# Hybrid stream step on one core: the first four columns projected without the adaLN shift, which is added to their results

## The chip, the cores and the metric

The kernel runs on one core of a Trainium2 chip. The metric is the device time of one execution in microseconds (us). Before the change it is 1371.86 us, the median of 3 runs (1371.81 to 1372.82).

## The reference, cut to what matters

One layer of an encoder is computed for 512 prompt rows and 64 sample rows (576 rows, 1024 channels). The two groups have their own conditioning vector c, and so their own shift, scale and gate.

```python
def layer(x, c, ...):
    mod = (jax.nn.silu(c) @ w_ada + b_ada)[:, None, :]
    sh1, sc1, gt1, sh2, sc2, gt2 = jnp.split(mod, 6, axis=-1)
    h = rms_normalize(x) * g_norm_mix * (1.0 + sc1) + sh1
    q, k, v, qi, ki, wi, z, xbc, dt, gate_logits = jnp.split(h @ w_in, offs, axis=-1)
    ...
    g_attn, g_ssm = jnp.split(jax.nn.sigmoid(gate_logits), 2, axis=-1)
    mixed = (g_attn * (o_attn @ w_branch_attn) + g_ssm * (y @ w_branch_ssm)) @ w_out
    x = x + gt1 * mixed
    ...
    return x, k, v, ki, ...
```

Between the projection and `mixed` stand a sparse attention, whose keys are chosen by an indexer (qi, ki, wi) with a top-k mask, and a state-space scan; after them a feed-forward layer follows. All of it is float32.

## The kernel before

**Order.** The kernel is not issued in the order of its text. A planner (class `Plan`) records each operation with its engine, an estimated cost and the buffers that it reads and writes, then makes one static order for each engine: whenever an engine is free in its model, it takes the ready operation with the smallest priority, which is the operation's place in the text minus an offset (`R.prio(4000)` pulls an operation forward by 4000 places, `R.prio(-1500)` pushes it back). Each engine then works through its list in order and waits at an instruction whose inputs are late. DMAs are issued on SP's queue in such an order too, so one that waits holds back all behind it. Since the planner emits everything, nearly every row of the profile has the same line, L533, and is told from others by its tile names: `out<-in`.

**Exact products.** Each float32 factor is split into a rounded half and the remainder (`hTh` and `hTl` for h, `wh` and `wl` for the weights), and a product is three matmuls: high·high, low·high, high·low. The weights come as 512 KB blocks (`raw`, two buffers), are split by ACT (`wh<-raw`) and DVE (`wl<-raw,wh`), with three buffers each.

**The head.** `build` begins with the conditioning: `sil` holds silu(c) in columns of 32, of which two are used, for prompt and sample. x comes in five row tiles `xt`. ACT squares and sums them, POOL makes 1/rms (`rs`), DVE scales (`xn`), PE transposes the scaled rows, and ACT copies them to `xnT` (channels on partitions, 8 tiles `kt` of 128 channels by 576 rows). The unscaled rows are transposed too (`mm<-ident,xt`), copied to `xs` and later stored to `x_d` for the residual.

`ada_pair(j)`, j = 0 to 3, loads the shift and the scale columns of 256 channels (four loads of 512 KB, tile `adr`), multiplies them in 32 matmuls on 32 columns of the array, copies the result (`ra`), transposes it, adds the bias (`modc`) and makes `A1` = (1 + scale)·g. `h_tile(kt)` makes u = xnT·A1 + shift (`hu`; DVE for even kt, ACT for odd), `hTh` (ACT) and `hTl` (DVE, for every fourth kt POOL). `hsS` holds copies of the 64 sample rows.

**The first products.** With channels on the output partitions ("feature-major", 288 columns a matmul) come `misc` (104 columns: indexer key, indexer weights and dt) and NE = 2 gate columns, the second of which is accumulated in the `px` and `py` banks. The results go to `mT` and, through a tanh, as `sg` to `gate_d` in DRAM. Then come "token-major" products (`tm`, 256 columns a matmul) for the indexer's queries (qi), k, v and q. `mT` is transposed to `misc`, a rotary table `cs2` (printed `cs`), the gains `gqk`, the products of both (`tabs`, on POOL) and the cached indexer keys `kisd` are loaded at this place. The remaining gate columns and z columns (`fillers`) are spread through the attention: PE works on them while DVE makes the top-k masks.

**The fifth modulation block.** The half of gt1 with u = 4 is made by `ada_columns(4, adx, 1, 1, 1)` in a pool of its own: 16 operations on DVE accumulate c·w_ada row block by row block in `aacc`, and 16 matmuls with `pick` sum over the partitions.

The names that the change and the prediction touch: `fetch` and `load_raw` (weights), `ada`, `ada_pair`, `ada_columns`, `bcast_rows` (transposes a column of row values to all partitions), `h_tile`, `fm`, `fm_half`, `tm`, `fillers`, and the pools `sp` (closed when the head is done), `hp`, `adp` and `xsp`.

Of the kernel before, what the change touches and what calls it, by code (L numbers as in the profile page):

```python
# [5 lines left out]
F32 = mybir.dt.float32  # L6
# [3 lines left out]
OP = mybir.AluOpType  # L10
# [232 lines left out]
NADX = 1  # L243
NRAW, NWH = 2, 3
# [296 lines left out]
def build(tc, I, O):  # L541
# [35 lines left out]
    def load_raw(src, nk, n):  # L577
        raw = wp.tile([P, nk, n], F32, name=f"raw{cnt[0]}", tag="raw", bufs=NRAW)
        sync.dma_start(raw, src)
        return raw  # L580
# [20 lines left out]
    raws, outs, outs_made = {}, {}, []  # L601
# [10 lines left out]
    def fetch(done, limit=1 << 30):  # L612
# [6 lines left out]
        with R.prio(4000 if done or limit > 99 else 0):  # L619
            more = True  # L620
            while more:
                more = False
                j = state["ld"]
                if j < min(len(queue), limit) and j < state["sp"] + NRAW:
                    i, s = queue[j]
                    if s == "misc":
                        raw = wp.tile([P, 8, 104], F32, name="rawm", tag="raw", bufs=NRAW)
                        sync.dma_start(raw[:, :, 0:72], kview(w_in[:, C_KI:C_KI + 72]))
                        sync.dma_start(raw[:, :, 72:104], kview(w_in[:, C_DT:C_DT + 32]))
                        raws[j] = (raw, 8, 104)  # L630
                    else:
                        raws[j] = (load_raw(*s), s[1], s[2], 27 <= j < 48)
# [15 lines left out]
    NE = 2  # L648
# [82 lines left out]
    def ada_pair(j):  # L731

        p = px(f"pada{j}", "py")
        for k4 in range(2):
            raw = [sp.tile([P, 4, 256], F32, name=f"wada{j}{k4}{w}", tag="adr", bufs=8) for w in range(2)]
            for w in range(2):
                sync.dma_start(raw[w], kview(w_ada[512 * k4:512 * k4 + 512, D * w + 256 * j:D * w + 256 * j + 256]))
            for i in range(4):
                kt = 4 * k4 + i
                for g in range(4):  # L740
                    pe.matmul(p[32 * g:32 * g + 32, 0:P], sil[:, kt, :], raw[g // 2][:, i, P * (g % 2):P * (g % 2) + P],
                              start=(kt == 0), stop=(kt == 7), tile_position=(0, 32 * g))
# [4 lines left out]
        for w in range(2):  # L747
            vec.tensor_tensor(modc[:, w, 2 * j:2 * j + 2, :], p2[:, 64 * w:64 * w + 64].rearrange("p (g s) -> p g s", g=2)[:, :, 0:2],
                              badc[:, 8 * w + 2 * j:8 * w + 2 * j + 2, None].to_broadcast([P, 2, 2]), OP.add)
        vec.scalar_tensor_tensor(A1[:, 2 * j:2 * j + 2], sc1[:, 2 * j:2 * j + 2], 1.0, g_mix[:, 2 * j:2 * j + 2, None].to_broadcast([P, 2, 2]),  # L750
                                 op0=OP.add, op1=OP.mult)
# [53 lines left out]
    xnT = sp.tile([P, 8, T], F32, name="xnT")  # L805
# [3 lines left out]
    for tb in range(5):  # L809
        n = P if tb < 4 else NS  # L810
        xn = sp.tile([P, D], F32, name=f"xn{tb}", tag="xn", bufs=2)
        act.activation(xn[:n], xt[tb][:n], AF.Square, accum_out=rs[:n, tb:tb + 1])
        rstd_of(rs[:n, tb:tb + 1], rs[:n, tb:tb + 1], 1, n, D)
        vec.tensor_scalar(xn[:n], xt[tb][:n], rs[:n, tb:tb + 1], None, op0=OP.mult)
        for k4 in range(2):
            p = px(f"pxn{tb}_{k4}")
            for j in range(4):
                kt = 4 * k4 + j
                pe.transpose(p[:, j * P:j * P + n], xn[:n, kt * P:(kt + 1) * P], ident[:n, :n])
            act.activation(xnT[:, 4 * k4:4 * k4 + 4, tb * P:tb * P + n], p.rearrange("p (k q) -> p k q", k=4)[:, :, :n], AF.Copy)  # L820
# [22 lines left out]

    A1 = cp.tile([P, 8, 2], F32, name="A1")
# [4 lines left out]
    def h_tile(kt):  # L849
        u = sp.tile([P, T], F32, name=f"hu{kt}", tag="hu", bufs=3)  # L850
        for s, c0, n in PARTS:
            if kt % 2:
                act.activation(u[:, c0:c0 + n], xnT[:, kt, c0:c0 + n], AF.Identity, bias=sh1[:, kt, s:s + 1], scale=A1[:, kt, s:s + 1])
            else:
                vec.tensor_scalar(u[:, c0:c0 + n], xnT[:, kt, c0:c0 + n], A1[:, kt, s:s + 1], sh1[:, kt, s:s + 1], op0=OP.mult, op1=OP.add)
# [5 lines left out]
    for j in range(4):  # L861
        ada_pair(j)
        fetch(0, EARLY[j])
        h_tile(2 * j)
        h_tile(2 * j + 1)
    for t, src in ((dtb, "dt_bias"), (alg, "a_log"), (dsk, "d_skip")):
        sync.dma_start(t, I[src].to_broadcast([P, 32]))
    for k4 in range(2):
        ks = slice(4 * k4, 4 * k4 + 4)
        act.activation(hsS[:, ks, 0:NS], hTh[:, ks, NP_:T].bitcast(F32), AF.Copy)  # L870
        act.activation(hsS[:, ks, NS:P], hTl[:, ks, NP_:T].bitcast(F32), AF.Copy)
    xst = []
    with R.prio(-1500):
        for tb in range(5):
            n = P if tb < 4 else NS
            p = pmm(f"pxt{tb}")
            for kt in range(8):
                pe.transpose(p[:, kt // 4, (kt % 4) * P:(kt % 4) * P + n], xt[tb][:n, kt * P:(kt + 1) * P], ident[:n, :n])
            st = xsp.tile([P, 8, P], F32, name=f"xs{tb}", tag="xs", bufs=5)
            for k4 in range(2):  # L880
                vec.tensor_copy(st[:, 4 * k4:4 * k4 + 4, :n], p[:, k4].rearrange("p (k q) -> p k q", k=4)[:, :, :n])
            if tb < 4:
                xst.append((x_d[:, :, tb // 2, tb % 2 * P:tb % 2 * P + P], st))
            else:
                for hf in range(2):
# [1212 lines left out]
```

## Time and profile before

| | us |
|---|---|
| median of 3 runs | 1371.86 |
| the profiled execution | 1372.06 |
| its span, first to last instruction | 1370.4 |
| busy: PE / DVE / ACT / POOL | 1351.5 / 1112.8 / 735.8 / 250.8 |

All durations in the text are from the one profiled execution; the runs' median stands for the time. The matmuls are pipelined: one shows about 0.3 us of its own, while the next begins some 0.13 us after it. A row of a timeline has start, length, engine, line, operation, tiles and count, and in brackets how long the engine sat idle before it and who released it. The granted TensorE clock was 0.999.

### The profile page before, as it was taken

How to read it: one execution, taken by the hardware profiler on the slowest of the kernel's cores; microseconds unless marked ns; L12 is line 12 of the kernel's file. 1: busy time of each engine (PE TensorE's matmuls, PEld its weight loads, DVE VectorE, ACT ScalarE, POOL GpSimd, SP SyncE). 2: the span in 40 equal slices, each digit the busy share in tenths (PEclk: the TensorE clock that was granted, in tenths of full speed). 3: DMA queues.
4: the chain of work that ended last, by engine and by line, in shares of the span. 5: the costliest groups of instructions: out<-in, count | busy, mean ns of one | idle time of the engine just before them, and what ended most of it. 6: DMA issues, size and time to landing. Idle time of an engine off the chain costs nothing.

```text
span 1370.4 us, 27779 instructions
## 1 busy us (share of the span) xinstructions
PE 1351.5 (99%) x10705; PEld 1312.5 (96%) x10705; DVE 1112.8 (81%) x2249; ACT 735.8 (54%) x1535; POOL 250.8 (18%) x376
## 2 busy tenths in 40 slices
PE   7999999999999999999999999999999999999998
PEld 5899999999999999999999999999999999999998
DVE  5688999787778698888897588868799998878564
ACT  5435343777876666666665342224576666664321
POOL 1312002230300245546453200001000000000000
PEclk9999999999999999999999999999999999999999
DMA  9762335574754644444445598757233343325431
GB/s 297 225 177 84 110 106 149 129 190 99 178 143 112 175 127 122 138 129 139 132 116 170 179 310 264 241 158 254 91 94 100 105 133 94 93 74 158 122 107 36
DMA packets 267764, 200.70 MB, mean 146 GB/s; under 512 B 25200, under 2 KB 239376, under 8 KB 267632
## 3 DMA queue, kind: packets, MB, share of 16 engines
q1 hardware_dynamic: 263680, 184.77, 46.0%
q0 software_dynamic: 3952, 14.16, 5.0%
q8 instruction: 84, 1.38, 0.4%
q14 instruction: 48, 0.39, 0.1%
HBM read 158.33 MB, written 29.55 MB: 137 GB/s over the span
## 4 chain that ended last, share of the span: by engine, by line
PE 86%; DVE 7%; DMA 4%; ACT 2%; issue 1%; SPq 1%; ACTq 0%; DVEq 0%
PE mm L533 61%; PE py L533 14%; PE px L533 11%; DMA stage<-y_d 2%; DVE score L533 1%; DMA raw<-in_w_in 1%; DVE m L533 1%; DVE wl L533 1%; SPq L533 1%; DMA xt<-in_x_sample 1%; DVE y L533 0%; ACT wh L533 0%; DVE xlS L533 0%; DMA rawu<-in_w_gate_up 0%; ACT wl L533 0%
## 5 line engine op out<-in xcount | busy, mean ns | idle before, releaser
L533 ACT ACTIVATE wh<-raw 128x1024 fp32r<-128x1024 f32 (+3 forms) x152 | 149.0, 983 | 181.4 <-PE mm L533 117.4
L533 PE MATMUL mm<-hTh,wh 128*128 128x288 f32 (+1 forms) x1024 | 235.5, 305 | 0.9 <-ACT hTh L533 0.9
L533 PE MATMUL mm<-hTh,wl 128*128 128x288 f32 (+1 forms) x1024 | 232.0, 301 | 0.0
L533 PE MATMUL mm<-hTl,wh 128*128 128x288 f32 (+1 forms) x1024 | 230.0, 301 | 0.4 <-DVE hTl L533 0.4
L533 PEld LDWEIGHTS mm<-hTh,wh 128*128 128x128 f32 (+1 forms) x1024 | 166.7, 188 | 3.9 <-ACT hTh L533 1.5
L533 PEld LDWEIGHTS mm<-hTh,wl 128*128 128x128 f32 (+1 forms) x1024 | 166.3, 188 | 2.7 <-issue 1.6
L533 PEld LDWEIGHTS mm<-hTl,wh 128*128 128x128 f32 (+1 forms) x1024 | 165.4, 188 | 3.3 <-issue 1.2
L533 DVE TENSOR_TENSOR wl<-raw,wh 128x1024 fp32r<-128x1024 f32 (+2 forms) x109 | 132.4, 1215 | 27.7 <-ACT wh L533 24.3
L533 DVE SCALAR_TENSOR_TENSOR cu<-xc,wc,cu 128x579 f32<-128x579 f32 x96 | 83.6, 870 | 2.1 <-ACT cu L533 1.6
L533 PE MATMUL mm<-wl,hTh 128*128 128x256 f32 x256 | 72.4, 284 | 0.0
L533 PE MATMUL mm<-wh,hTl 128*128 128x256 f32 x256 | 72.3, 284 | 0.0
L533 PE MATMUL mm<-wh,hTh 128*128 128x256 f32 x256 | 72.0, 284 | 0.0
L533 DVE SCALAR_TENSOR_TENSOR aacc<-adr,sil,aacc 128x512 f32<-128x512 f32 x84 | 59.8, 754 | 4.4 <-DMA adr<-in_w_ada 4.1
L533 PE MATMUL mm<-yh,wl 128*128 128x288 f32 x256 | 56.2, 298 | 0.0
L533 PE MATMUL mm<-yh,wh 128*128 128x288 f32 x256 | 55.2, 298 | 0.5 <-ACT yh L533 0.5
L533 PE MATMUL mm<-yl,wh 128*128 128x288 f32 x256 | 54.8, 296 | 0.6 <-DVE yl L533 0.6
L533 ACT ACTIVATE P<-lg,mn 128x128 f32<-128x128 f32 (+4 forms) x72 | 41.7, 581 | 25.2 <-DVE mn L533 24.0
L533 PE MATMUL mm<-xhS,wh 128*128 128x290 f32 (+1 forms) x248 | 55.2, 297 | 0.0
L533 PE MATMUL mm<-xhS,wl 128*128 128x290 f32 (+1 forms) x232 | 51.2, 296 | 0.0
L533 ACT ACTIVATE dec<-dec,nacs 128x128 f32<-128x128 f32 x128 | 42.5, 392 | 13.5 <-POOL dec L533 12.9
L533 PEld LDWEIGHTS mm<-wl,hTh 128*128 128x128 f32 x256 | 48.2, 189 | 0.4 <-issue 0.2
L533 PEld LDWEIGHTS mm<-wh,hTl 128*128 128x128 f32 x256 | 48.1, 188 | 0.3
(509 smaller groups left out, 3978.3 us busy)
## 6 DMA issues: line engine op xcount, KB each, us to landing
raw<-in_w_in SPq DMA_DIRECT2D x80, 512.0 KB, 4.0
adr<-in_w_ada SPq DMA_DIRECT2D x36, 512.0 KB, 5.2
raw<-in_w_gate_up SPq DMA_DIRECT2D x22, 512.0 KB, 3.8
wl<-raw POOLq DMA_DIRECT2D x21, 512.0 KB, 4.7
rawu<-in_w_gate_up SPq DMA_DIRECT2D x20, 512.0 KB, 3.9
bc<-acs_d SPq DMA_DIRECT2D x32, 256.0 KB, 3.6
raw<-in_w_branch_ssm SPq DMA_DIRECT2D x16, 512.0 KB, 4.5
raw<-in_w_down SPq DMA_DIRECT2D x16, 448.0 KB, 3.9
```

Of the source, the lines that this page charges most:

```text
L533: getattr(engines[x.eng], x.fn)(*[real(a) for a in x.args], **{k: real(v) for k, v in x.kw.items()})
```

## The change

h is linear in the shift, so h @ w = (x·rs·A1) @ w + shift @ w.

- **Scale first.** `ada_scale(j)` loads only the scale columns (two loads of 512 KB, the two halves of the channels of c beside each other on the array; six `adr` buffers in place of eight), and adds both halves after the transposition.
- **x once.** The unscaled rows are transposed once, into `xT`; x_d is stored from there. `rs` is transposed and broadcast to `rB`, and `xr` = xT·rB on DVE takes the place of `xnT`.
- **Two passes over h.** `h_tile(kt, 0)` makes h without the shift. From it come four early columns: misc and NE = 3 gate columns, whose unsplit weights are kept (`raw_early`). Then `h_tile(kt, 1)` makes h anew with the shift, into the same `hTh` and `hTl`, for all later products.
- **The shift's own products.** `ada(0)` and `ada(1)` make the shift by matmuls on four loads of 512 KB each (pulled forward by SHP = 1000). 32 matmuls multiply it with the four kept weight blocks, and the result, copied (`rashift`), transposed and scaled (`shiftw`), enters as a bias: of two ACT operations that make `mT`, and of six tanh for the three gate columns. These now go to `gate_d` in one stretch, ahead of `cs2`, `gqk` and the cached keys in the text.
- **The fifth block.** `ada(4)` by 32 matmuls takes the place of `ada_columns(4)`, its pool and its 16 DVE operations.
- **One filler less.** With NE = 3 the third gate column is no longer among the fillers. `fetch` pulls weight splits forward only after the early columns.

```diff
...
+NADR = 6
+SHP = 1000
...
-    def load_raw(src, nk, n):
-        raw = wp.tile([P, nk, n], F32, name=f"raw{cnt[0]}", tag="raw", bufs=NRAW)
+    def load_raw(src, nk, n, first=None):
+        raw = wp.tile([P, nk, n], F32, name=f"raw{cnt[0]}", tag="raw", bufs=NRAW) if first is None else sp.tile([P, nk, n], F32, name=f"rawE{first}")
...
-    raws, outs, outs_made = {}, {}, []
+    raws, outs, outs_made, raw_early = {}, {}, [], []
...
-        with R.prio(4000 if done or limit > 99 else 0):
+        with R.prio(4000 if done > NE else 0):
...
-                        raw = wp.tile([P, 8, 104], F32, name="rawm", tag="raw", bufs=NRAW)
+                        raw = sp.tile([P, 8, 104], F32, name="rawE0")
...
-                        raws[j] = (load_raw(*s), s[1], s[2], 27 <= j < 48)
+                        raws[j] = (load_raw(*s, j if j < NE + 1 else None), s[1], s[2], 27 <= j < 48)
+                    if j < NE + 1:
+                        raw_early.append(raws[j][0])
...
-    NE = 2
+    NE = 3
...
-    def ada_pair(j):
+    def ada_scale(j):
...
-        for k4 in range(2):
-            raw = [sp.tile([P, 4, 256], F32, name=f"wada{j}{k4}{w}", tag="adr", bufs=8) for w in range(2)]
-            for w in range(2):
-                sync.dma_start(raw[w], kview(w_ada[512 * k4:512 * k4 + 512, D * w + 256 * j:D * w + 256 * j + 256]))
-            for i in range(4):
-                kt = 4 * k4 + i
-                for g in range(4):
-                    pe.matmul(p[32 * g:32 * g + 32, 0:P], sil[:, kt, :], raw[g // 2][:, i, P * (g % 2):P * (g % 2) + P],
-                              start=(kt == 0), stop=(kt == 7), tile_position=(0, 32 * g))
+        raw = [sp.tile([P, 4, 256], F32, name=f"wada{j}{h}", tag="adr", bufs=NADR) for h in range(2)]
+        for h in range(2):
+            sync.dma_start(raw[h], kview(w_ada[512 * h:512 * h + 512, D + 256 * j:D + 256 * j + 256]))
+        for i in range(4):
+            for h in range(2):
+                for t in range(2):
+                    g = 2 * h + t
+                    pe.matmul(p[32 * g:32 * g + 32, 0:P], sil[:, 4 * h + i, :], raw[h][:, i, P * t:P * t + P],
+                              start=(i == 0), stop=(i == 3), tile_position=(0, 32 * g))
...
-        for w in range(2):
-            vec.tensor_tensor(modc[:, w, 2 * j:2 * j + 2, :], p2[:, 64 * w:64 * w + 64].rearrange("p (g s) -> p g s", g=2)[:, :, 0:2],
-                              badc[:, 8 * w + 2 * j:8 * w + 2 * j + 2, None].to_broadcast([P, 2, 2]), OP.add)
-        vec.scalar_tensor_tensor(A1[:, 2 * j:2 * j + 2], sc1[:, 2 * j:2 * j + 2], 1.0, g_mix[:, 2 * j:2 * j + 2, None].to_broadcast([P, 2, 2]),
-                                 op0=OP.add, op1=OP.mult)
+        m = modc[:, 1, 2 * j:2 * j + 2, :]
+        halves = [p2[:, 64 * h:64 * h + 64].rearrange("p (g s) -> p g s", g=2)[:, :, 0:2] for h in range(2)]
+        vec.tensor_tensor(m, halves[0], badc[:, 8 + 2 * j:8 + 2 * j + 2, None].to_broadcast([P, 2, 2]), OP.add)
+        vec.tensor_tensor(m, m, halves[1], OP.add)
+        vec.scalar_tensor_tensor(A1[:, 2 * j:2 * j + 2], m, 1.0, g_mix[:, 2 * j:2 * j + 2, None].to_broadcast([P, 2, 2]), op0=OP.add, op1=OP.mult)
...
-    xnT = sp.tile([P, 8, T], F32, name="xnT")
+    xT = xsp.tile([P, 8, T], F32, name="xT")
+    xr = sp.tile([P, 8, T], F32, name="xr")
...
-        xn = sp.tile([P, D], F32, name=f"xn{tb}", tag="xn", bufs=2)
-        act.activation(xn[:n], xt[tb][:n], AF.Square, accum_out=rs[:n, tb:tb + 1])
+        sq = sp.tile([P, D], F32, name=f"xsq{tb}", tag="xsq", bufs=1)
+        act.activation(sq[:n], xt[tb][:n], AF.Square, accum_out=rs[:n, tb:tb + 1])
...
-        vec.tensor_scalar(xn[:n], xt[tb][:n], rs[:n, tb:tb + 1], None, op0=OP.mult)
+        p = pmm(f"pxt{tb}")
+        for kt in range(8):
+            pe.transpose(p[:, kt // 4, (kt % 4) * P:(kt % 4) * P + n], xt[tb][:n, kt * P:(kt + 1) * P], ident[:n, :n])
...
-            p = px(f"pxn{tb}_{k4}")
-            for j in range(4):
-                kt = 4 * k4 + j
-                pe.transpose(p[:, j * P:j * P + n], xn[:n, kt * P:(kt + 1) * P], ident[:n, :n])
-            act.activation(xnT[:, 4 * k4:4 * k4 + 4, tb * P:tb * P + n], p.rearrange("p (k q) -> p k q", k=4)[:, :, :n], AF.Copy)
+            vec.tensor_copy(xT[:, 4 * k4:4 * k4 + 4, tb * P:tb * P + n], p[:, k4].rearrange("p (k q) -> p k q", k=4)[:, :, :n])
...
+    pr = bcast_rows("prx", rs)
+    rB = sp.tile([P, T], F32, name="rB")
+    act.activation(rB[:, 0:NP_], pr[0], AF.Copy)
+    act.activation(rB[:, NP_:T], pr[1][:, 0:NS], AF.Copy)
...
-    def h_tile(kt):
-        u = sp.tile([P, T], F32, name=f"hu{kt}", tag="hu", bufs=3)
+    def h_tile(kt, shift):
+        if not shift:
+            vec.tensor_tensor(xr[:, kt], xT[:, kt], rB, OP.mult)
+        u = sp.tile([P, T], F32, name=f"hu{kt}{shift}", tag="hu", bufs=3)
...
+            a, b = A1[:, kt, s:s + 1], sh1[:, kt, s:s + 1]
...
-                act.activation(u[:, c0:c0 + n], xnT[:, kt, c0:c0 + n], AF.Identity, bias=sh1[:, kt, s:s + 1], scale=A1[:, kt, s:s + 1])
+                act.activation(u[:, c0:c0 + n], xr[:, kt, c0:c0 + n], AF.Identity, bias=b if shift else 0.0, scale=a)
...
-                vec.tensor_scalar(u[:, c0:c0 + n], xnT[:, kt, c0:c0 + n], A1[:, kt, s:s + 1], sh1[:, kt, s:s + 1], op0=OP.mult, op1=OP.add)
+                vec.tensor_scalar(u[:, c0:c0 + n], xr[:, kt, c0:c0 + n], a, b if shift else None, op0=OP.mult, **({"op1": OP.add} if shift else {}))
...
-        ada_pair(j)
+        ada_scale(j)
...
-        h_tile(2 * j)
-        h_tile(2 * j + 1)
+        h_tile(2 * j, 0)
+        h_tile(2 * j + 1, 0)
...
-    for k4 in range(2):
-        ks = slice(4 * k4, 4 * k4 + 4)
-        act.activation(hsS[:, ks, 0:NS], hTh[:, ks, NP_:T].bitcast(F32), AF.Copy)
-        act.activation(hsS[:, ks, NS:P], hTl[:, ks, NP_:T].bitcast(F32), AF.Copy)
...
-    with R.prio(-1500):
-        for tb in range(5):
-            n = P if tb < 4 else NS
-            p = pmm(f"pxt{tb}")
-            for kt in range(8):
-                pe.transpose(p[:, kt // 4, (kt % 4) * P:(kt % 4) * P + n], xt[tb][:n, kt * P:(kt + 1) * P], ident[:n, :n])
-            st = xsp.tile([P, 8, P], F32, name=f"xs{tb}", tag="xs", bufs=5)
-            for k4 in range(2):
-                vec.tensor_copy(st[:, 4 * k4:4 * k4 + 4, :n], p[:, k4].rearrange("p (k q) -> p k q", k=4)[:, :, :n])
-            if tb < 4:
-                xst.append((x_d[:, :, tb // 2, tb % 2 * P:tb % 2 * P + P], st))
-            else:
-                for hf in range(2):
-                    xst.append((x_d[:, :, hf, HP:TH], st[:, :, HS * hf:HS * hf + HS]))
+    for tb in range(4):
+        xst.append((x_d[:, :, tb // 2, tb % 2 * P:tb % 2 * P + P], xT[:, :, tb * P:tb * P + P]))
+    for hf in range(2):
+        xst.append((x_d[:, :, hf, HP:TH], xT[:, :, NP_ + HS * hf:NP_ + HS * hf + HS]))
...
+    early = []
+    for e in range(NE + 1):
+        w = getw()
+        m = w[0][0].shape[2]
+        if e == 2:
+            ps = [px(f"pe{e}{hf}", ("px", "py")[hf])[:, :TH] for hf in range(2)]
+            for k in range(8):
+                for hf in range(2):
+                    fm_half([ps[hf]], w, hh, hl, hf, (k,))
+        else:
+            ps = fm(f"pe{e}", w, hh, hl)
+            ps = [ps[:, hf] for hf in range(2)]
+        t = sp.tile([P, T], F32, name=f"early{e}")
+        with R.prio(4000):
+            for hf in range(2):
+                (act.activation(t[:m, hf * TH:hf * TH + TH], ps[hf], AF.Copy) if hf else
+                 vec.tensor_copy(t[:m, hf * TH:hf * TH + TH], ps[hf]))
+        early.append(t)
+    with R.prio(SHP):
+        ada(0, sp, NADR)
+        ada(1, sp, NADR)
+    with R.prio(0):
+        ada(4, sp, NADR)
+    shz = sp.tile([P, 8, 32], F32, name="shz")
+    pool.memset(shz, 0.0)
+    vec.tensor_copy(shz[:, :, 0:2], sh1)
+    p = px("pshift", "py")
+    order = [1, 2, 3, 0]
+    for kt in range(8):
+        for g, e in enumerate(order):
+            n = 104 if e == 0 else P
+            pe.matmul(p[32 * g:32 * g + 32, 0:n], shz[:, kt], raw_early[e][:, kt, :n], start=(kt == 0), stop=(kt == 7), tile_position=(0, 32 * g))
+    ra = sp.tile([P, P], F32, name="rashift")
+    pool.memset(ra, 0.0)
+    vec.tensor_copy(ra[:, 0:104], p[:, 0:104])
+    vec.tensor_copy(ra[0:96, 104:P], p[0:96, 104:P])
+    p2 = px("pshiftT", "py")
+    pe.transpose(p2[:, 0:P], ra, ident)
+    shiftw = adp.tile([P, 4, 2], F32, name="shiftw")
+    cols = p2[:, 0:P].rearrange("p (g s) -> p g s", g=4)[:, :, 0:2]
+    vec.tensor_scalar(shiftw[:, 0:3], cols[:, 0:3], 0.5, None, op0=OP.mult)
+    vec.tensor_copy(shiftw[:, 3:4], cols[:, 3:4])
+    for kt in range(8):
+        h_tile(kt, 1)
+    for k4 in range(2):
+        ks = slice(4 * k4, 4 * k4 + 4)
+        act.activation(hsS[:, ks, 0:NS], hTh[:, ks, NP_:T].bitcast(F32), AF.Copy)
+        act.activation(hsS[:, ks, NS:P], hTl[:, ks, NP_:T].bitcast(F32), AF.Copy)
+    gate_d = R.dram([16, P, T], F32, name="gate_d")
+    z_d = R.dram([P, 16, T], F32, name="z_d")
+    mT = hp.tile([104, T], F32, name="mT")
+    for s, c0, n in PARTS:
+        act.activation(mT[:, c0:c0 + n], early[0][:104, c0:c0 + n], AF.Identity, bias=shiftw[:104, 3, s:s + 1])
+    for e in range(1, NE + 1):
+        for s, c0, n in PARTS:
+            act.activation(early[e][:, c0:c0 + n], early[e][:, c0:c0 + n], AF.Tanh, bias=shiftw[:, e - 1, s:s + 1], scale=0.5)
+        sync.dma_start(gate_d[e - 1], early[e])
...
-    gate_d = R.dram([16, P, T], F32, name="gate_d")
-    z_d = R.dram([P, 16, T], F32, name="z_d")
-    nfs = []
+    nfs = list(range(NE))
...
-            if nf == 1 and n == NE:
-                w = getw()
-                halves = [px(f"pf{nf}{hf}", ("px", "py")[hf])[:, :TH] for hf in range(2)]
-                for k in range(8):
-                    for hf in range(2):
-                        fm_half([halves[hf]], w, hh, hl, hf, (k,))
-                sg = ap_.tile([P, T], F32, name=f"sg{nf}", tag="sg", bufs=bufs)
-                for hf in range(2):
-                    act.activation(sg[:, hf * TH:hf * TH + TH], halves[hf], AF.Tanh, scale=0.5)
-                sync.dma_start(gate_d[nf], sg)
-                continue
...
-    mT = ap_.tile([104, T], F32, name="mT", tag="lg", bufs=4)
-    ps = fm("pmisc", getw(), hh, hl)
-    fillers(NE)
-    act.activation(mT.rearrange("p (a b) -> p a b", a=2), ps, AF.Copy)
...
-    adx = R.mkpool("adax", side="right", reuse_waits="tile")
-    with R.prio(0):
-        ada_columns(4, adx, 1, 1, 1)
-    R.close(adx)
...
```

## The prediction

> **What bounds the kernel now.** I read the page first, then busy time by stretches, then the chain of waits and the queues inside the stretch that stands out.
>
> ```profile
> span 1370.4 us, 27779 instructions
> PE 1351.5 (99%) x10705; PEld 1312.5 (96%) x10705; DVE 1112.8 (81%) x2249; ACT 735.8 (54%) x1535; POOL 250.8 (18%) x376
> PE   7999999999999999999999999999999999999998
> ```
>
> TensorE idles for 1370.4 − 1351.5 = 18.9 us in all. Whatever the change does to ACT, DVE or the loads pays only through those gaps, or through matmuls added and removed.
>
> ```profile
> 0.00:28.80 28.80, 19.64 (x217) 15.98 (x217) 13.92 (x34) 15.07 (x28) 5.74 (x20) 1.00 0.98 292
> 28.80:57.00 28.20, 27.08 (x277) 23.34 (x276) 17.29 (x33) 14.39 (x25) 9.03 (x12) 1.00 0.86 247
> 57.00:100.00 43.00, 42.87 (x371) 42.01 (x370) 36.41 (x59) 15.27 (x28) 7.62 (x5) 1.00 0.66 187
> 100.00:200.00 100.00, 99.52 (x769) 97.47 (x770) 95.69 (x205) 43.40 (x77) 8.96 (x6) 1.00 0.35 100
> ```
>
> Columns: length, then busy time of PE, PEld, DVE, ACT, POOL, granted clock, DMA share, GB/s. The gaps of the head are 9.16 + 1.12 us; there the DMA engines are full (0.98). From 57 on PE has 42.87 of 43. The clock is 1.00, so it plays no part. From 100 on DVE has 95.69 of 100 and could become the bound.
>
> ```profile
> 3.43 7.62 DMA xt<-in_x_sample
> 31.49 6.56 DMA raw<-in_w_in
> 44.25 1.00 PE py L533 x28
> 46.85 1.15 ACT hu L533 x2
> 48.61 2.13 DVE hTl L533 x2
> ```
>
> The chain of waits through the head goes from load to load, to the last modulation block (44.25), and through hu, hTh and hTl to 50.74; the matmuls of the last h tiles follow and PE is not released from outside again.
>
> **The head by parts.** Loads first.
>
> ```profile
> 32.08 4.86 SPq L533 DMA_DIRECT2D adr<-in_w_ada  x4
> 36.00:40.00 4.00, 3.46 (x26) 2.83 (x24) 2.30 (x7) 1.93 (x3) 0.00 (x0) 1.00 1.11 343
> adr<-in_w_ada SPq DMA_DIRECT2D x16, 512.0 KB, 7.4
> ```
>
> The last of 16 half-MB modulation loads is issued just before 36.94 and lands 7.4 later at about 44, where its matmuls run. x landed at 3.43 + 7.62 = 11.05. Between lie 16 × 0.524 + misc 0.43 + two gate columns 1.05 = 9.87 MB in 33 us, 300 GB/s; up to the gate column that lands at 31.49 + 6.56 = 38.05 it was 8.3 MB in 27 us, 307. The change keeps every byte, but the shift half of the loads goes behind. Ahead of the last scale load stand 8 scale loads 4.19, misc and two columns 1.48, and, as its order puts them, the four loads of ada(0), 2.10: 7.77 MB, 25.3 to 25.9 us, so 36.4 to 37.0. At the 334 GB/s that lie near the best stretch (343 from 36 to 40) it would be 34.3. I take 36.0, nearer to the two averages, 8 us sooner than 44.
>
> Second, the one transposition.
>
> ```profile
> L533 PE MATMUL px<-ident,xn 128*128 128x128 f32 (+1 forms) x40 | 5.8, 295 | 1.3 <-DVE rs L533 0.9 <-DVE xn L533 0.4
> L533 ACT ACTIVATE xnT<-px 128x512 f32<-128x512 f32 (+1 forms) x10 | 5.1, 552 | 6.7 <-PE px L533 6.7
> ```
>
> These 40 transposes (5.8 us) and 10 copies (5.1) go, with the 5 scalings; 5 broadcasting transposes, 2 copies and 8 products xT·rB come (576 columns with two inputs, priced below as an hTl, 0.7 each, 5.7). All lies before 36, in the 9.16 us that PE idles while loads fill the queues: nothing on the path. Without that cover it would gain some 3 us.
>
> Third, the chain behind the last scale load, from these rows:
>
> ```profile
> 45.30 0.29 DVE L533 COPY ra<-py 128x128 f32<-128x128 f32 x1 [4.10 <-PE py L533]
> 33.23 1.43 DVE L533 TENSOR_TENSOR hTl<-hu,hTh 128x576 fp32r<-128x576 f32 x2 [1.04 <-ACT hTh L533]
> 48.61 2.12 DVE L533 TENSOR_TENSOR hTl<-hu,hTh 128x576 fp32r<-128x576 f32 x2 [0.44 <-ACT hTh L533]
> 54.47 0.29 PE L533 MATMUL px<-hTl,wh 128*128 128x288 f32 x1
> 56.60 0.30 PE L533 MATMUL py<-hTh,wl 128*128 128x288 f32 x1
> 61.72 0.28 PE L533 MATMUL mm<-wh,hTl 128*128 128x256 f32 x1
> 64.44 0.28 PE L533 MATMUL mm<-wl,hTh 128*128 128x256 f32 x1
> ```
>
> Modulation block 1.0 and ra to hTl (45.30 to 50.73) 5.4, with one more small addition: 6.55, so hTl7 at 42.55. Sixteen starts from 54.47 to 56.60 give 0.133 us per 288-column matmul; 23 from 61.72 to 64.44 give 0.118 per 256-column one. Then in the changed order: 30 matmuls 4.0, ada(1)'s block 1.35 (1.0 for 28, a row above), the last 24 of the third column 3.2, the 48 of the new fourth column 6.4: its end lies at 57.55.
>
> **The second pass.** Only then may the last h tiles be overwritten with the shifted ones.
>
> ```profile
> 46.85 1.15 ACT L533 ACTIVATE hu<-xnT,modc,A 128x512 f32<-128x512 f32 x2 [0.39 <-DVE A L533]
> 47.90 1.25 ACT L533 ACTIVATE hTh<-hu 128x576 fp32r<-128x576 f32 x2
> 49.18 0.42 ACT L533 ACTIVATE hsS<-hTh 128x256 fp32r<-128x256 f32 x1
> 52.83 1.05 ACT L533 ACTIVATE wh<-raw 128x1024 fp32r<-128x1024 f32 x1
> 56.53 0.41 ACT L533 ACTIVATE sg<-px 128x288 f32<-128x288 f32 x1 [2.11 <-PE px L533]
> ```
>
> On ACT, wh of the next weights waits for that column's end, and behind it in order stand a copy, hu5, hTh5, hTh4, hTh6, hu7, hTh7 and two hsS: 1.05 + 0.41 + 2 × 1.15 + 4 × 0.62 + 2 × 0.42 = 7.1. With hTl7 0.7 on DVE and hand-overs of 0.4 PE gets its last tile 8.2 after 57.55, at 65.75. It has 27 token-major matmuls (3.2), ada(4) and 32 shift products (1.35 and 1.15) in this time: some 2.4 us of new idling.
>
> Before reaches the same work at 56.74 (its second gate column ends there) + 27 × 0.118 = 3.2 + the third gate column, a filler until now, 6.4 + the sums of ada(4):
>
> ```profile
> 56.74 0.52 PE L533 MATMUL px<-ident,lg 104*128 104x104 f32 x4
> L533 PE MATMUL px<-aacc,pick x16: 272/285/297, 98.8 to 99.7; 128*32 128x128 f32 x16
> L533 DVE SCALAR_TENSOR_TENSOR aacc<-adr,sil,aacc x14: 736/741/1268, 55.5 to 95.7; 128x512 f32<-128x512 f32 x14
> ```
>
> 98.8 to 99.7 and a transpose, with grouping 1.6: in all 67.9. The 16 DVE sums (0.74 each, 12 us) cost nothing now, since from 57 to 100 DVE is busy 36.41 of 43 and PE does not wait; taking them away gains nothing either.
>
> Last, what SP issues behind the gate stores.
>
> ```profile
> 43.32 0.37 SPq L533 DMA_DIRECT2D cs<-in_rope  x1
> kisd<-in_cache_ki SPq DMA_DIRECT2D x2, 128.0 KB, 4.5
> ```
>
> The static order puts three gate stores, each behind its tanh, ahead of cs, gqk and the cached keys. The stores end some 4 us after the last tile (2 copies to mT, 6 tanh at 0.2 to 0.6 each), the keys issue near 72 and land 4.5 later, near 76.5. PE reaches their transposes some 9.5 us after 65.75: a wait of 1.2, between 0 and 4. mT's transposes add 0.3. Queued behind it on PE are the rest of the token-major columns; on DVE wl of the next weights stands behind a rope product that waits for cs.
>
> Sum: 65.75 + 1.2 + 0.3 = 67.25 against 67.9, a gain of 0.65. The profiled execution's own time, 1372.06, is 0.2 above the median 1371.86; against the median I forecast **1371.2**.
>
> A look at sharing between POOL and DVE, for its own sake:
>
> ```profile
> 49.04 6.74 POOL L533 TENSOR_TENSOR tabs<-cs,gqk 128x320 f32<-128x320 f32 x6 [0.52 <-DMA gqk<-in_g_q]
> 76.80 3.36 DVE L533 SCALAR_TENSOR_TENSOR e<-e,e 128x160 f32<-128x160 f32 x2
> 82.81 0.31 DVE L533 SCALAR_TENSOR_TENSOR e<-e,e 128x160 f32<-128x160 f32 x1
> 77.02 2.96 POOL L533 TENSOR_TENSOR tok<-tok,cs 128x1280 f32<-128x1280 f32 x1 [14.58 <-DVE tmpb L533]
> ```
>
> Two operations of 0.31 took 3.36 beside a POOL product of 2.96, and the hTl pair at 48.61 took 2.12, not 1.43, as the tables began at 49.04. The Trainium skill, page "SBUF — State Buffer", section "🔬 SBUF: two separate sides", says that a DVE operation with two SBUF inputs and a GpSimd one that reads SBUF lock each other out for the whole instruction; the rows agree, and by it the tables moved behind the gate stores could hold DVE up to 6.74 us more, 1371.2 + 6.7 = 1377.9 if PE waited for all of it.
>
> **The rivals.** (a) The new waits vanish: the last scale load lands at 34.3 (−1.7), ACT's tail runs under the fourth column (−2.4 of idling) and the keys are in time (−1.2). For it: ACT is busy only 14.39 of 28.20 in this stretch. Against: wh and the copies stand in front of hu by order. 1371.2 − 5.3 = 1365.9.
>
> (b) Slower: the late group cs, gqk, keys. gqk lands near 76, the six tables (6.74) then run beside DVE, and wl of the next weights, behind the rope product, comes late to PE. The price: the keys' wait at its upper end (+2.8) and a two-input wl held behind about two of the six tables (2 × 1.12 = 2.2): 1371.2 + 5.0 = 1376.2. It decides once PE's waits for kisd and wl together pass 3.5 us. For it: the collision rows; against: three wl buffers ahead.
>
> (c) Slower: the mask stage.
>
> ```profile
> L533 ACT ACTIVATE lg<-py x32: 377/458/602, 116.7 to 187.9; 128x288 f32<-128x288 f32 x8, 128x256 f32<-128x256 f32 x8, 128x384 f32<-128x384 f32 x8, 128x512 f32<-128x512 f32 x8
> 247.62 0.33 PE L533 MATMUL py<-kst,qst 128*128 128x128 f32 x2
> ```
>
> The first logits come at 116.7, and the gate column that now stands ahead of them (6.4 us) was cover for the DVE work behind them. If DVE is the limit until 247.62, half of it turns up as PE idling: 1371.2 + 3.2 = 1374.4. Against: other products take the column's place there, 131 us of matmuls as before.
>
> (d) The change does not free the head: the last scale load, behind ada(0), lands as late as now. Then 44 − 36 = 8 us come on top: 1379.2.
>
> **How the numbers follow.** Forecast 0.40, with its own range 1368 to 1374.5 (landing 34.3 to 37.0; keys' wait 0 to 4); (a) 0.27, (b) 0.20, (c) 0.10, (d) 0.03. 0.2% is 2.7 us, 1369.1 to 1374.6, about what a measurement of this kernel can tell from no change. Of the forecast's 0.40, 0.09 falls under that and 0.06 above; of (c) 0.03 stays within. Faster 0.27 + 0.09 = 0.36, slower 0.06 + 0.20 + 0.07 + 0.03 = 0.36, within 0.25 + 0.03 = 0.28. The range takes (a) and (b) with a margin of about 1.5: 1364.5 to 1378.
>
> **What would show it.** Right: the last block of scale matmuls near 36, hTl7 of the first pass near 42.5, PE gaps of 2 to 3 us between 57 and 66, one of about 1 at the kisd transposes, tables on POOL after 72, q·k within 3 us of 247.6. Wrong: scale matmuls at 40 or later (d); no gap between 57 and 77 (a); PE released by DVE wl or DMA kisd for over 3.5 us near 70 to 80 (b); PE idle between 190 and 250 (c).

## The result, and the profile after

The changed kernel takes 1385.09 us (median of 4, 1383.09 to 1386.25) against 1372.34 beside it: ratio 1.0087, 95% interval 1.0073 to 1.0101. It is slower by about 12.7 us, and outside the predicted range. Of the runs below one execution, of p2_fifth_mm, is left out: it took 1453.29 us at a granted clock of 0.85. The profiled execution is the one of 1386.25; its page begins:

```profile
span 1384.4 us, 27974 instructions
PE 1356.2 (98%) x10785; PEld 1315.0 (95%) x10785; DVE 1119.6 (81%) x2263; ACT 739.3 (53%) x1550; POOL 255.8 (18%) x380
PE   6999999999999999999999999999999999999998
```

TensorE is busy 4.7 us longer and idles 28.2 us, 9.3 more than before. Busy time by stretches of the changed kernel, with the columns of the prediction:

```profile
0.00:28.80 28.80, 16.11 (x118) 11.68 (x118) 15.19 (x38) 10.99 (x19) 4.73 (x21) 1.00 0.83 240
28.80:57.00 28.20, 28.16 (x331) 25.58 (x328) 15.06 (x33) 11.49 (x20) 3.91 (x4) 1.00 0.93 303
57.00:100.00 43.00, 41.17 (x427) 39.63 (x426) 25.68 (x51) 24.03 (x45) 13.40 (x14) 1.00 0.50 149
```

Up to 28.8 TensorE works less than before (16.11 against 19.64), and the DMA engines are no longer full (0.83 against 0.98). The hole lies between 24 and 28 us. SP's queue waits for TensorE before it, 6.9 us up to 25.96: the next loads need one of the six `adr` buffers, and the block of modulation matmuls at 24.00 frees them as it ends. The first row is the stretch (DMA share and GB/s at its end), the second SP's waits up to 45 us (total, times, longest), the third the same in the kernel before, with eight buffers:

```profile
24.00:28.00 4.00, 1.93 (x33) 1.38 (x32) 4.00 (x11) 1.34 (x3) 0.00 (x0) 1.00 0.21 35
SPq L535 <- PE py L535: 17.2, 4, 6.9
SPq L533 <- PE py L533: 6.7, 4, 2.5
```

From 28.8 to 57 TensorE does not idle at all: no load holds it up there. Its rows in the head of the changed kernel (start, length, tiles, count):

```profile
13.17 1.97 PE L535 MATMUL mm<-ident,xt 128*128 128x128 f32 x8 [0.79 <-DVE rs L535]
19.77 1.94 PE L535 MATMUL py<-adr,sil 128*32 128x128 f32 x32
23.62 0.45 PE L535 MATMUL py<-ident,ra 128*128 128x128 f32 x1 [1.91 <-DVE ra L535]
24.00 1.94 PE L535 MATMUL py<-adr,sil 128*32 128x128 f32 x32
30.41 1.92 PE L535 MATMUL py<-adr,sil 128*32 128x128 f32 x28
42.73 1.07 PE L535 MATMUL py<-adr,sil 128*32 128x128 f32 x28
45.99 1.96 PE L535 MATMUL py<-adr,sil 128*32 128x128 f32 x64
53.08 1.96 PE L535 MATMUL py<-adr,sil 128*32 128x128 f32 x64
64.97 1.95 PE L535 MATMUL py<-adr,sil 128*32 128x128 f32 x64
68.72 1.95 PE L535 MATMUL py<-rawE,shz 128*32 128x128 f32 x64
72.24 0.33 PE L535 MATMUL py<-ident,rashift 128*128 128x128 f32 x1 [0.43 <-DVE rashift L535]
85.09 0.63 PE L535 MATMUL px<-ident,kisd 128*128 128x128 f32 x4 [1.01 <-DMA kisd<-in_cache_ki]
```

and the kernel before at the same work:

```profile
10.54 1.91 PE L533 MATMUL px<-ident,xn 128*128 128x128 f32 x8
13.71 1.04 PE L533 MATMUL px<-ident,xn 128*128 128x128 f32 x8
20.77 1.08 PE L533 MATMUL py<-adr,sil 128*32 128x128 f32 x32
44.18 1.07 PE L533 MATMUL py<-adr,sil 128*32 128x128 f32 x28
```

Two things stand there. First, a row of 32 takes 1.94 at 20 and 24 us, and 1.08 in the kernel before: up to about 34 us TensorE goes at half its pace. Second, a block of ada (32 matmuls in the code) shows as 64 rows and 1.95 us at full pace; four of them now stand between 46 and 70 us, where TensorE has no idle time to hide them.

To place the loss I use a *lag*: how much later an execution has done the same products as the kernel before had at a given time. It is worked out from all TensorE rows of the two traces, each product counted with one price per shape; modulation and shift products and the transposes of x are not counted, and all kernels have the same total. The changed kernel's lag is −2.2 at 44 us (it leads), 1.6 at 57, 9.2 at 85, 9.8 at 230, 13.7 at 320 and 13.9 at 1300. So 11.4 us are lost between 44 and 85, and 3.9 between 230 and 320. The figures at 44 and 57 us move by up to 1 us with the prices chosen, those from 85 on by 0.2 at most. The longest wait between 230 and 320, on TensorE of the changed kernel, then the scalings of P on VectorE (first in the kernel before, then in the changed one) and what POOL did there:

```profile
300.14 0.63 PE L535 MATMUL py<-kst,qst 128*128 128x512 f32 x2
302.28 0.77 PE L535 MATMUL px<-ident,P 128*128 128x128 f32 x4 [1.50 <-DVE P L535]
```

```profile
276.25 1.41 DVE L533 TENSOR_SCALAR P<-P,sm 128x384 f32<-128x384 f32 x4
299.90 3.31 DVE L535 TENSOR_SCALAR P<-P,sm 128x384 f32<-128x384 f32 x4
```

```profile
299.09 2.92 POOL L535 TENSOR_TENSOR tok<-tok,tabs 128x1280 f32<-128x1280 f32 x1 [0.53 <-DVE tmpb L535]
```

Four scalings of P that took 1.41 in the kernel before take 3.31 beside a POOL product of 2.92, and TensorE waits 1.50 for them. Before, the same POOL product ran from 292.1 without such a wait. Nothing of the change touches these instructions: they meet because the static order behind the head is another one.

### The profile page after: what moved, and what is told of

It is laid out like the page before. It is cut to its first block, busy times and chain, and to the rows that moved or that the text cites. A ratio compares the mean times of both kernels' runs of the same rounds, so it can differ in the third digit from the quotient of the medians.

```text
span 1384.4 us, 27974 instructions
## 1 busy us (share of the span) xinstructions
PE 1356.2 (98%) x10785; PEld 1315.0 (95%) x10785; DVE 1119.6 (81%) x2263; ACT 739.3 (53%) x1550; POOL 255.8 (18%) x380
## 4 chain that ended last, share of the span: by engine, by line
PE 77%; DVE 7%; DMA 7%; issue 4%; ACT 4%; POOL 1%; SPq 0%; ACTq 0%; POOLq 0%
PE mm L535 53%; PE py L535 13%; PE px L535 10%; DVE score L535 2%; DMA stage<-y_d 2%; DMA wl<-raw 2%; DMA raw<-in_w_in 1%; DMA bc<-acs_d 1%; DVE m L535 1%; DVE wl L535 1%; ACT wh L535 1%; ACT dec L535 0%; DMA kisd<-in_cache_ki 0%; DVE xr L535 0%; DVE cu L535 0%
## 5 line engine op out<-in xcount | busy, mean ns | idle before, releaser
L535 ACT ACTIVATE wh<-raw 128x1024 fp32r<-128x1024 f32 (+2 forms) x148 | 145.1, 981 | 177.4 <-PE mm L535 115.4
L535 DVE TENSOR_TENSOR wl<-raw,wh 128x1024 fp32r<-128x1024 f32 (+1 forms) x105 | 126.6, 1206 | 31.3 <-ACT wh L535 28.7
L535 ACT ACTIVATE P<-lg,mn 128x128 f32<-128x128 f32 (+4 forms) x72 | 41.7, 580 | 24.1 <-DVE mn L535 23.6
L535 DVE SCALAR_TENSOR_TENSOR aacc<-adr,sil,aacc 128x512 f32<-128x512 f32 x70 | 49.3, 747 | 1.3 <-DMA adr<-in_w_ada 1.2
```

The source lines that it names most:

```text
L535: getattr(engines[x.eng], x.fn)(*[real(a) for a in x.args], **{k: real(v) for k, v in x.kw.items()})
```

## The experiments

Three theories: A, the four blocks cost their full price because TensorE is the bound there; B, the single transposition starts the head late, with TensorE at half pace and eight products on VectorE ahead of the first modulation; C, the second pass and the loads behind the gate stores cost the time. Later D: the new order of the later stages costs several us by itself. The lag of each profiled execution (one execution each, so a difference of about 1.5 means little; those of e3, o1 and s1 lie 3 us below their kernel's median, that of p1 3 us above):

| kernel | 44 | 57 | 85 | 230 | 320 | 1300 us | ratio to before, interval |
|---|---|---|---|---|---|---|---|
| the change | −2.2 | 1.6 | 9.2 | 9.8 | 13.7 | 13.9 | 1.0087, 1.0073 to 1.0101 |
| e1_warm | −5.1 | −1.4 | 5.1 | 5.6 | 12.0 | 10.8 | 1.0073, 1.0058 to 1.0088 |
| e2_fifth_dve | −3.4 | 0.4 | 5.8 | 12.6 | 20.6 | 23.6 | 1.0175, 1.0158 to 1.0192 |
| e3_two_transposes | −4.7 | −2.5 | 4.1 | 4.8 | 7.9 | 6.3 | 1.0069, 1.0051 to 1.0086 |
| e4_eighth | −3.8 | −1.6 | 1.3 | 0.5 | −0.2 | 3.7 | 1.0033, 1.0020 to 1.0046 |
| e5_keys_first | −3.3 | 0.4 | 6.8 | 6.0 | 9.9 | 10.8 | 1.0084, 1.0068 to 1.0100 |
| p1_once | 5.1 | 5.3 | 5.3 | 5.3 | 5.3 | 6.1 | 1.0030, 1.0021 to 1.0040 |
| p2_fifth_mm | 2.9 | 5.6 | 7.4 | 5.7 | 8.1 | 8.6 | 1.0055, 1.0033 to 1.0076 |
| p3_ne3 | 1.6 | 1.0 | 1.0 | 1.4 | 8.2 | 13.6 | 1.0084, 1.0066 to 1.0102 |
| o1_before_order | 0.0 | −1.4 | −1.4 | −1.1 | −1.3 | 0.2 | 1.0019, 1.0005 to 1.0033 |
| o2_after_order | −2.2 | 1.6 | 9.1 | 9.3 | 11.9 | 11.1 | 1.0074, 1.0059 to 1.0089 |
| c1_two_fifth | −5.4 | −3.1 | 1.9 | 9.0 | 15.8 | 18.8 | 1.0139, 1.0121 to 1.0156 |
| c2_ne2 | −2.7 | 7.4 (0.6 just ahead of a wait) | 10.0 | 8.7 | 10.5 | 14.8 | 1.0099, 1.0080 to 1.0118 |
| s1_two_eighth | −5.0 | −3.8 | −0.8 | −1.6 | −1.3 | 1.2 | 1.0025, 1.0011 to 1.0040 |
| v1_two_order | −4.9 | −2.6 | 4.1 | 4.7 | 6.9 | 6.2 | 1.0042, 1.0025 to 1.0059 |

**e1_warm**, the changed kernel with idle time filled:

```diff
+    pwarm = px("pwarm", "py")
+    def warm(n, ops=()):
+        with R.prio(-100000), R.after(ops):
+            for _ in range(n):
+                pe.transpose(pwarm[:, 0:P], ones, ident)
+    warm(16)
...
+        warm(8, [last])
```

> The changed kernel with 56 transposes of the ones tile added, 16 before x arrives and 8 behind each x tile, in TensorE's idle time; their results are not used. Theory B (the halved transposes leave TensorE at half pace until 34.3 us, and this holds up the whole head): the pace of a transpose doubles by about 10 us, h without the shift is ready 3 to 5 us sooner, and the time falls from 1385.1 to 1380 to 1382. Theory A (TensorE is bound by the four modulation and shift blocks that now stand among the first products, 1.95 us each): the start changes, the time by less than 1.5 us. Theory C (the second pass and the late loads cost the time): no change beyond 1.5 us.

1382.77. TensorE of e1_warm:

```profile
19.72 1.08 PE L535 MATMUL py<-adr,sil 128*32 128x128 f32 x32
22.49 1.08 PE L535 MATMUL py<-adr,sil 128*32 128x128 f32 x32
```

56 useless transposes make the same block at the same time take 1.08 instead of 1.94, and the lead at 44 grows from 2.2 to 5.1. The whole falls by some 2.3, less than theory B gave: the pace is a part of the loss, about 3 us of lag, not the larger one. The times alone don't settle it, since their intervals overlap: in this run TensorE waits 3.02 for `qst` up to 262, and 6.4 of lag are lost between 230 and 320 in place of 3.9.

**e2_fifth_dve**, the fifth block back on VectorE:

```diff
-    with R.prio(0):
-        ada(4, sp, NADR)
...
+    adx = R.mkpool("adax", side="right", reuse_waits="tile")
+    with R.prio(0):
+        ada_columns(4, adx, 1, 1, 1)
+    R.close(adx)
```

> The changed kernel with the fifth modulation block back on VectorE, in its old place. Theory A: one block of 1.95 us leaves the stretch in which TensorE does not idle, and the 16 summing matmuls (about 0.9 us) come back: 1383.5 to 1384.3. Theory C: the block runs in TensorE's waits of the second pass and costs nothing, so no change or up to 1 us slower, 1385 to 1386. Theory B: no change.

1395.94, far from all three. From 44 to 85 the lag grows by 9.2 instead of 11.4, 2.2 for one block, as theory A has it. Then it jumps by 6.8 between 130 and 230. The sums in e2_fifth_dve (durations min/median/max, first and last start):

```profile
L535 DVE SCALAR_TENSOR_TENSOR aacc<-adr,sil,aacc x14: 737/743/3253, 86.0 to 135.8; 128x512 f32<-128x512 f32 x14
```

Before they ran from 55.5 to 95.7, ahead of the first logits. Here their pool opens later, they reach into the mask stage, and TensorE waits for their result (1.66 at 139.5) and for what stands behind them on VectorE (1.26 at 141.7). Behind these waits it goes at half pace: the granted clock is 0.50 from 143 to 147. With this head the block could not stay where it was.

**e3_two_transposes**, the single transposition undone:

```diff
-    xT = xsp.tile([P, 8, T], F32, name="xT")
-    xr = sp.tile([P, 8, T], F32, name="xr")
+    xnT = sp.tile([P, 8, T], F32, name="xnT")
...
+        vec.tensor_scalar(xn[:n], xt[tb][:n], rs[:n, tb:tb + 1], None, op0=OP.mult)
...
-            vec.tensor_tensor(xr[:, kt], xT[:, kt], rB, OP.mult)
```

> The changed kernel with x transposed twice again (scaled on VectorE before, as in the kernel before); all else stays. Theory B: TensorE reaches full pace near 13 us as before, VectorE is rid of the eight products of 0.67 us in front of the first modulation, and the time falls by 3 to 6 us, to 1379 to 1382. Theories A and C: the 40 transposes come back where TensorE idles, 1384 to 1386.

1381.82, 3.3 less than the change, and a lag at 85 of 4.1 instead of 9.2. Theory B holds for this part. The intervals of the two times overlap, so the size of the gain rests on the lag and on p1_once below.

**e4_eighth**, the blocks cut to one eighth:

```diff
-            for kt in range(8):
+            for kt in (range(7, 8) if u in (0, 1, 4) else range(8)):
...
-    for kt in range(8):
+    for kt in range(7, 8):
         for g, e in enumerate(order):
```

> The changed kernel with one eighth of the matmuls of ada(0), ada(1), ada(4) and of the shift's products: seven of eight rows of channels are left out of the sums, the loads stay. Theory A: 4 x 1.7 = 6.8 us less, 1378 to 1379. Theory C: TensorE waits for the second pass and the keys instead, at most 2 us less, 1383 to 1385. Theory B: as theory C.

1376.55, 8.5 less. From 44 to 85 the lag grows by 5.1 instead of 11.4: 6.3 where 6.8 were taken off TensorE. Theory A holds, and theory C, which left the time to other waits, falls for these 6 us. The later loss came elsewhere (4.6 between 460 and 480), in yet another order.

**p1_once**, the kernel before with x transposed once (the edit is that of the change's third bullet: `xT`, `rB`, `xr`).

> The kernel before with x transposed once (xT, rB, xr) and nothing else of the change. Theory B (fewer transposes keep TensorE cold, and eight products stand on VectorE ahead of the modulation): the first h tiles come 2 to 5 us later and the whole time grows by 2 to 5 us, 1374 to 1377. Rival, as predicted (all of it lies under the loads): within 1.5 us of 1372.

1376.48, ratio 1.0030. TensorE of p1_once:

```profile
19.88 3.64 PE L533 MATMUL py<-adr,sil 128*32 128x128 f32 x64
26.63 1.76 PE L533 MATMUL py<-adr,sil 128*32 128x128 f32 x32
32.34 1.71 PE L533 MATMUL py<-adr,sil 128*32 128x128 f32 x28
```

The pace is half up to 34 us, and the lag of 5.3 stays within 0.1 from 57 to 480: nothing behind the head gives it back. The loads suffer too: SP waits 7.1 us for A where it waited 2.6, and the DMA share is 0.07 from 32 to 36 (1.06 before). What I had put at nothing costs some 4 us by itself.

**p2_fifth_mm**, the kernel before with the fifth block by matmuls:

```diff
+    with R.prio(0):
+        ada(4, sp, 8)
     R.close(sp)
...
-        ada_columns(4, adx, 1, 1, 1)
```

> The kernel before with the fifth modulation block by 32 matmuls in the head and nothing else of the change. Theory A (the head does not idle behind the loads any more when the block comes): +1.95 for the block, -0.9 for the sums, so 1372.5 to 1374. Theory D (what a new static order does to the attention stage is worth several us, whatever was changed): the work-for-work lag against the kernel before jumps by 2 us or more somewhere between 130 and 500 us, and the time is 1374 to 1382.

Ratio 1.0055. The block comes between 50 and 65 (3.5 of lag), its sums give back 2.0 between 85 and 116, and 2.4 are lost between 230 and 320. More than theory A's 1 us, and a part of it by a head that is 2.9 late at 44, which I did not follow up.

**p3_ne3**, the kernel before with three early gate columns:

```diff
-    NE = 2
+    NE = 3
...
-    fillers(NE)
     act.activation(mT.rearrange("p (a b) -> p a b", a=2), ps, AF.Copy)
+    fillers(NE)
```

> The kernel before with a third gate column among the first products (NE = 3; the copy of misc's result stands ahead of the gate columns in the text) and nothing else of the change. Rival (c) of the prediction (the column was cover for the mask stage): lag that grows between 116 and 250 us, 3 us or more, 1375 to 1379. Theory D: lag that jumps in the first attention blocks between 250 and 500 us. Neither: within 1.5 us of 1372, no jump.

1385.19 with a lag of 1.4 at 230. All the loss is in two jumps, 6.7 between 247 and 260 and 6.2 between 460 and 480. The largest wait of TensorE around the first, from 247 to 262 us (us in total, times, longest):

```profile
PE mm L533 <- DMA wl<-raw: 3.5, 1, 3.5
```

So rival (c), lost cover in the mask stage, falls: the stage itself is as long as before. A weight load that lands late in the new order makes half of this jump, and TensorE's pace behind it some more:

```profile
253.01 0.28 PE L533 MATMUL mm<-wh,hTl 128*128 128x256 f32 x1
256.90 0.58 PE L533 MATMUL mm<-wl,hTh 128*128 128x256 f32 x1 [3.49 <-DMA wl<-raw]
258.56 0.41 PE L533 MATMUL mm<-wh,hTh 128*128 128x256 f32 x1
258.78 0.41 PE L533 MATMUL mm<-wl,hTh 128*128 128x256 f32 x1
258.00:262.00 4.00, 4.00 (x27) 4.00 (x27) 1.67 (x7) 2.43 (x8) 0.92 (x1) 0.72 0.57 146
```

The products follow each other after 0.21 us instead of 0.12 up to 260.8, which costs some 1.5 us (an estimate from these starts), and the granted clock is 0.72.

**e5_keys_first**, the table and the cached keys ahead of the gate stores:

```diff
+    cs2 = kp.tile([P, 5, P], F32, name="cs2")
+    sync.dma_start(cs2, I["rope"])
+    kisd = kp.tile([P, 9, 2, HD], F32, name="kisd")
...
     xst = []
```

> The changed kernel with the rotary table and the cached indexer keys loaded ahead of the gate stores (the squares of x go into xr's place to make room). Rival (b) of the prediction: TensorE's wait for the keys (1.0 us) goes, and the lag at 85 us falls from 9.2 by 1 to 2 us; 1382 to 1384. Theory A: the wait goes, 1.0 us and no more; later jumps are another order's.

1384.78. From 44 to 85 the lag grows by 10.1 instead of 11.4: the wait of 1.0 is gone, and little more. It is gone in e1, e3, e4 and c2 as well, where TensorE comes to the keys at another time. Rival (b) falls as the main cause.

**o1_before_order** and **o2_after_order**, the same instructions in another order from the masks on:

```diff
-        op.slack = self.slack if eng == "tensor" else 0.0
+        op.slack = self.slack + self.more if eng == "tensor" else 0.0
...
+    R.more = 0.05
     masks = []
```

> The kernel before with the planner's margin behind TensorE 0.30 instead of 0.25 us for the instructions from the top-k masks on: the same instructions, the head in the same order, the stages behind it in another. Theory D (the order behind the head is worth several us, and the kernel before has a good one): no lag up to 110 us, then jumps of 1 to 5 us; 1374 to 1378. Rival (the order is worth nothing, the jumps of the other kernels come from their changes): within 1 us of 1372.

> The changed kernel with the same margin changed in the same place. Theory D: the lag of 9.8 at 230 us stays, the three waits between 260 and 320 us (3.5 us together) go or others come, so 1381 to 1389. Rival: the same three waits and 1384 to 1386, since the change itself sets them.

The kernel before gets slower (1375.56 beside 1373.12, ratio 1.0019). Its executions go from 1372.68 to 1381.60, and the profiled one is the fastest, so no trace shows where the time goes. The changed kernel takes 1383.70, but its interval overlaps that of the change, so a gain is not shown. In its trace the lag of 9.3 at 230 stays, and 2.6 instead of 3.9 are lost up to 320. For the kernel before theory D holds in kind: an order alone cost some 2 us (0.7 to 4.5 by the interval). It doesn't explain jumps of 6.

**c1_two_fifth** (e3 and e2 together) and **c2_ne2** (the changed kernel with `NE = 2`, `order = [1, 2, 0]`):

> The changed kernel with both undone: x transposed twice, the fifth block on VectorE. What is left is the early columns without the shift, the shift's products and NE = 3. Theories A and B together: the lag at 85 us falls from 9.2 by 5.2 and 3.4 to about 0.6, and by 150 us some 2 of it come back with the sums. What the later order does is not foreseen: 1372 to 1385.

> The changed kernel with NE = 2: two early gate columns, the third is a filler again. Theory A: the blocks stay, so the lag at 85 us stays at 8 to 10; if the second pass was hidden by the third column, 1 to 3 us more. Rival (c) of the prediction (the column is missing as cover behind the first logits): the lag between 250 and 320 us does not grow, 1380 to 1382.

c1_two_fifth leads by 5.4 at 44, lags 1.9 at 85, and then loses 7 with the sums in the mask stage, as e2_fifth_dve did: 1391.89. c2_ne2 takes 1386.92. Its lag at 85 is about the same (10.0), though it gets there in another way: TensorE waits 1.31 and 0.71 near 60, and the block behind takes 3.39 instead of 1.95. With the third column there these waits don't come, so the column hid some of them; 1.8 instead of 3.9 are lost between 230 and 320, but 4 more come after 500.

**s1_two_eighth** (e3 and e4 together) and **v1_two_order** (e3 with o2's margin):

> The changed kernel with x transposed twice again, and one eighth of the matmuls of ada(0), ada(1), ada(4) and of the shift's products (the rest of these sums is left out). If the cost of the blocks (8.0 us of lag at 85 us) and that of the single transposition (5.2) lie one behind the other, the lag at 85 us is 9.2 - 8.0 - 5.2 = -4.0: the scale-first loads then gain 4 us that the rest eats, and the whole takes 1367 to 1373. If they overlap (a later start fills the same waits), the lag at 85 us is 0 to -2 and the whole takes 1372 to 1377.

> The changed kernel with x transposed twice and the planner's margin of 0.30 us from the masks on. The two gains seen alone (about 3.3 and 1.4 us) add up: 1379 to 1381. If the order's gain hung on the changed kernel's own head: 1381 to 1384.

s1_two_eighth takes 1376.42, with a lag of −0.8 at 85: the costs overlap. It leads by 5.0 at 44 and by 3.8 at 57, so the scale-first loads do gain about 5; then it loses 3 between 57 and 85 with hardly a block in the way. TensorE's only longer wait there is 0.70 for `rashift`, so it does not wait for the second pass even here; what makes up the rest is not shown. v1_two_order takes 1378.16, 1.0042 of the kernel before. It is the fastest form of the change that leaves nothing out; no version beat the kernel before.

## Why the prediction was wrong, point by point

- **The last scale load.** Forecast to land at 36.0. Its issue (the last of four) and the median landing time in the changed kernel's head are

```profile
27.40 5.97 SPq L535 DMA_DIRECT2D adr<-in_w_ada  x4
```

```profile
adr<-in_w_ada SPq DMA_DIRECT2D x20, 512.0 KB, 5.5
```

  so it landed near 27.40 + 5.97 + 5.5 = 38.9, some 5 earlier than before. The forecast let the loads run at 300 GB/s without a break and had no term for the buffers, for which SP waited 17.2 us; no run with eight buffers tells what that cost. But the block's matmuls stand in TensorE's order at 38.24 (the first four rows) and 42.73 (the rest), with thirty products and no idle time between them: the load was not what set the head any more. The lead was 2.2 in the changed kernel, 3.3 to 3.8 in e2, e4 and e5, whose head is much the same, and 5 with TensorE at full pace (e1, e3, s1), not 8.
- **"All lies before 36 …: nothing on the path."** This step failed. The eight products xT·rB stand in VectorE's order between and ahead of the modulation's small operations, whose results TensorE waits for (1.91 at 23.62). And with 40 transposes fewer, TensorE goes at half pace to 34 us. Alone it costs 3.9 us (p1_once); undone, it gives back 3.3 (e3_two_transposes). It was called hidden by the idling of TensorE; that idling itself makes the later work slow. "The clock is 1.00, so it plays no part" was read from a column that does not show this (last section).
- **The blocks.** "ada(1)'s block 1.35 (1.0 for 28, a row above)" took the row of 28 for most of a block. Each of these matmuls shows as two rows (ada's 32 as 64), so that row is 14 matmuls, less than half of ada(1), whose block takes 1.96. The blocks of ada(1), ada(4) and the shift were given 1.35, 1.35 and 1.15, and that of ada(0) had no term at all: 3.85 of the 7.8 us that stand there.
- **"some 2.4 us of new idling" in the second pass, that takes in ada(4) and the shift products.** This is the step that failed most. (The terms beside it give 8.2 − 3.2 − 1.35 − 1.15 = 2.5, and the fourth column's end is 57.50; neither matters.) TensorE was behind by then: the fourth column ended at 64.97 instead of 57.55, and the blocks were work on the path, with waits of 0.4 for `ra` and `rashift` beside them. In no trace does TensorE wait between 57 and 77 for `hTh` or `hTl` of the second pass, not even with the blocks cut to an eighth (e4, s1).
- **The keys.** 1.2 forecast, 1.01 measured; the mechanism was right, though both sides came 8 us later than forecast (the keys issued at 79.62 instead of 72).
- **Rivals.** (a) did not come. (b) cost 1.0, not 5; the tables came late as foreseen, but TensorE waited only 0.5 for wl between 60 and 120. (c) fell with p3_ne3. (d) fell: the loads did come sooner.
- **What no rival had.** 3.9 us between 230 and 320, from waits in an order that the planner made anew. I had noted that much of the order changes, and priced the product work there (131 us) as equal; the waits were not in it.

As sums of lag: a lead of 5 by the loads, 3 of it lost by half pace; 7.8 for four blocks; 1.0 for the keys; 2.6 more up to 85 us; 0.6 to 230; 3.9 to 320. −5 + 3 + 7.8 + 1.0 + 2.6 + 0.6 + 3.9 = 13.9. The 2.6 are what is left over: 0.8 are the two waits of 0.4, and no run separates the rest. In e3_two_transposes, where TensorE doesn't wait for the keys, the lag grows from 44 to 85 by 8.8, the blocks and these two waits.

## What to carry to other kernels

Work that runs while an engine waits for loads is free only there. Putting it off to let the loads for the first products come first moves it to where the engine is the bound, and it then costs its full price; count its rows in the trace before giving it one. Where a planner makes the order, a kernel that was measured often stands on an order that suits it, and any edit pays for a new one as well; shifting one margin, with the instructions unchanged, gives a first idea of how much that is. And a wait of TensorE is not over when it ends: behind one of 3.5 us the next products went at half pace.

## What the hardware showed that was not expected

TensorE's pace depends on how busy it was just before. In the kernel before, transposes went from 1.91 to 1.04 per eight near 13 us, after rows of 3.04 and 1.91 with hardly a gap. In the changed kernel, rows of 1.97 with gaps of 0.8 to 2.2 us between them never brought it to full pace up to 34, some 6 us after TensorE stopped idling at 28.5. The same happens far behind the head: after the wait of 3.49 at 253 p3_ne3 goes at half pace for 3.9 us, and after that of 3.02 at 259 e1_warm does for 3. The Trainium skill, page "TensorE: Matmul & The Clock Gate", section "🔬 Part 1: The HAM clock gate (the "warmup" mystery)", says that the array's default clock is half and that about 3.4 us of sustained work release it; the rows agree in kind, but in the head gaps well under 3.4 us were enough to keep it slow.

The granted clock shows only a part of this. It reads 1.00 from 0 to 28.8 in the changed kernel, whose rows take double there. In p3_ne3 and e2_fifth_dve, where full pace was lost again, it reads 0.72 (258 to 262) and 0.50 (143 to 147). In these traces it shows a pace that falls, not one that has not yet risen. The spells also differ between executions of the same instructions: the block at 24 us took 1.94 in the changed kernel and 1.08 in the one execution of e4_eighth that was profiled:

```profile
19.58 1.94 PE L535 MATMUL py<-adr,sil 128*32 128x128 f32 x32
23.66 1.08 PE L535 MATMUL py<-adr,sil 128*32 128x128 f32 x32
```
